# A hybrid encoder step on one core: operand splits later behind their loads, late norms in place, and a final norm by segments

## The chip, the cores and the metric

The kernel runs as one program on one core of one Trainium2 chip. The metric is the device time of one execution in microseconds (us): the median over the runs shown, smaller is better. The engines are TensorE (PE in the profile, with its weight loads as PEld), VectorE (DVE), ScalarE (ACT), GpSimd (POOL) and SyncE (SP), which issues most DMAs.

## The reference

One layer over 2,048 prompt rows and 32 sample rows (T = 2,080 rows in all), float32, d_model 1,024, d_ff 2,816. A mixing part (band attention and gated linear attention on one input projection) is followed by a gated MLP with a causal convolution. Cut to its core:

```
z = (rmsnorm(x) * (1 + scale_m) + shift_m) @ w_in
ya = band_attention(q, k, v, rel_bias)                  # own chunk of 64 rows and 8 before
yb = rmsnorm(gla(q, k, v, log_a)) * silu(gb)            # linear attention, per-token state
merged = sigmoid(gate_a) * (ya @ w_br_a) + sigmoid(gate_b) * (yb @ w_br_b)
x = x + gate_m * rmsnorm(merged @ w_out, g_post_mix)
h = rmsnorm(x, g_pre_ffn) * (1 + scale_f) + shift_f
u = h @ w_up
y = b_dw + sum_j w_dw[j] * shifted(u, j)                # three taps over rows
a, g = split(y, 2)
x = x + gate_f * rmsnorm((gelu(a) * g) @ w_down, g_post_ffn)
```

The outputs are the rows x, the last keys and values, the linear attention's final states and the last rows of u.

## The kernel before

All activations are held transposed, with channels on the 128 partitions and rows along the free axis. Every float32 operand of a matmul is used as two parts: `split` has ACT copy it into a rounded high part, and DVE subtracts that to get the low part (`hi`, `lo`); `mm3` makes three matmuls of each product: hi·hi, hi·lo, lo·hi. So each operand costs a DMA load into a raw tile, an ACT copy and a DVE subtraction before PE can use it.

The stages by time in the profile:

- 0 to about 240 us: modulation vectors and the first norms; to about 1,350: the input projection, linear attention and attention. PE's gaps there are filled by a generator `fill()`: first the gate projections (`dense`, which calls `ahead(i)` as it goes), then `branch_b()`, the merge product yb @ w_br_b in five column blocks of eight m-steps. `branch_b` also loads the next weights: `load_wb(q)` for w_br_b, `load_half` for w_br_a and w_out; each issues its DMA and calls `split` at once.
- about 1,500 to 1,810: eight blocks of 260 rows (`NBLK`, `ND`): `merge` adds both branches, `project` multiplies by w_out. `project` copies each of eight results out of PSUM on ACT (line 1258), squares it (1260 for the first, 1263 after), and calls `step()` between products. `norms`, a generator in `queue`, then makes the residual and the next norm's modulated rows, h, eight channel tiles each, and stores both to DRAM (`x1T`, `h2T`). The last blocks' norms run late, within the feed-forward: `rstd_late` waits for a place among the feed-forward's matmuls, and `hold[0]` keeps it back to a chosen block.
- from 1,810: the feed-forward as Strassen-Winograd products. Rows form three parts p of two segments of 348 to 350 columns. There are twelve units: three for the up-projection (one a part, 22 blocks each), then nine for the down-projection (three parts by three groups of channels, four blocks each). One block (`block(u, m, ...)`) is seven products `prod` of twelve matmuls each (nine where a group has three channel tiles), into two PSUM tiles `ad` and `g`, with ACT copies between (lines 1814 `g`, 1824 `U2`, 1827 `P5`) since a product accumulates onto a copy of another. A block's last two products (`rest_ad`, `rest_g`) run in the next block.
- from 3,206: the final norm of the last part, and the stores.

In the feed-forward all five engines follow the order in which the code is written (`in_order[0]`); before it PE is ordered by hand and a scheduler orders the others, save instructions pinned by `keep_in_program_order`. What decides the written order is `side()`, called between products. It advances `at_step`, runs `run_due()` (work put off by `soon(n, f)`, n steps later), one `step()` of norms, one `hstep()` and up to two `next(wq)`, and last `pend()`, one step of a `post(p)`.

- `hstep()` advances `load_ops`: it loads a unit's fourteen half operands from h, or later from the activations, up to three ahead (two while a `post` is pending), and splits each: lines 1569 (ACT) and 1570 (DVE, a step later).
- `wq` is `weights()`: it loads columns of weights into eight raw buffers, makes their Winograd sums, and splits each: lines 1645 (ACT) and 1650 (DVE, a step later). An engine that comes to a split whose load has not landed waits, with all that is queued behind it.
- `prod` itself calls `next(wq)` or `hstep()` with `run_due()` until both of its operands exist in the written order.
- `post(p)` is the final norm of part p: statistics on PE, then for each of eight channel tiles a multiply (line 1944, DVE), a residual add (1948: POOL for parts 0 and 1), a load of the next residual rows x1, and a store (1871, SP) two steps later. `post(0)` and `post(1)` run inside units 6 and 9; `post(2)` is the end of the program.
- the feed-forward's first weights are split early: `first()`, the `step` of the last `project`, calls `next(wq)`.

The late modulation in `norms` multiplies into a tile of two buffers, whose reuse waits for the store:

```
h2 = d3.tile([128, ND], F32, name="h2", tag="h2", bufs=2)
mul.tensor_mul(h2, o[:, m], r)
```

Of the kernel before, what the change touches and what calls it, by code (L numbers as in the profile page):

```python
# [58 lines left out]
def encoder_step(ctx: ExitStack, tc: tile.TileContext, I, O):  # L59
# [791 lines left out]
    with ExitStack() as st:  # L851
# [219 lines left out]

        def load_half(w, src, k, half):
# [4 lines left out]
            split(w[0][k][:, cs], w[1][k][:, cs], raw)  # L1077

        def load_wb(q):

            for k in (0, 2):
                raw = wt.tile([128, 2, 256], F32, name="wbr", tag="wr")
                nc.sync.dma_start(raw, dap(I["w_br_b"], k * 128 * D + 256 * q, [[D, 128], [128 * D, 2], [1, 256]]))
                split(wb_[q][0][:, k:k + 2], wb_[q][1][:, k:k + 2], raw)
# [10 lines left out]
        def split_y(y, raws):  # L1095
            for k, raw in zip((0, 2), raws):
                split(y[0][:, k:k + 2], y[1][:, k:k + 2], raw)

        def ahead(i):

            if i == 1:
                yb0.append(raw_y(ybT, NB, 0))
            elif i == 2:
                split_y(yb_[0], yb0.pop())
            elif i == 3:
                load_wb(0)

        def branch_b():

            was = iter([(k, half) for half in range(2) for k in range(4)])  # L1110
            for b in range(5):
                cols = slice(NB * b, NB * b + NB)
                for m in range(KD):
                    ms = slice(128 * m, 128 * m + 128)
                    if b == 0 and m in (0, 2, 4):
# [15 lines left out]
                    for k in range(4):  # L1131
# [6 lines left out]
                        if b == 4 and k == 3:  # L1138
                            load_half(wo_, I["w_out"], m // 2, m % 2)

# [93 lines left out]

    def project(b, step):
# [15 lines left out]
        for m in range(KD):  # L1251
# [6 lines left out]
            nc.scalar.copy(o[:, m], p[:, :ND])  # L1258
# [59 lines left out]

    def run_due():
        for f in due.pop(0) if due else ():  # L1320
            f()
# [9 lines left out]
    def norms(b, t0, o, first):  # L1331
# [26 lines left out]
        def modulate(m):  # L1358
            h2 = d3.tile([128, ND], F32, name="h2", tag="h2", bufs=2)
# [27 lines left out]
        for m in range(KD):  # L1387
# [3 lines left out]
            if m < KD - 1:  # L1391
                yield
        if b < NBLK - 2:
# [48 lines left out]

    def sums(p):

        w = WP[p]
        for j in range(4):
# [11 lines left out]
            for i, v in ((0, x), (2, y)):  # L1458
                nc.sync.dma_start(dap(hT, ((4 * p + i) * 512 + 128 * j) * W, [[W, 128], [512 * W, 2], [1, w]]), v[:, :, :w])
            yield  # L1460
# [59 lines left out]
    def load_ops(todo):  # L1520
# [23 lines left out]
        ahead = [0]  # L1544

        def more():
# [63 lines left out]
    def weights():  # L1610
# [5 lines left out]
        at = {}  # L1616
        cur = -1

        def fetch():
            while todo and free and todo[0][0] <= cur + 1:  # L1620
                c, x = todo.pop(0)
                at[c, x] = i = free.pop(0)
                nc.sync.dma_start(raw(i, NK[cols[c][0]]), w_rows(*cols[c], x))
# [5 lines left out]
        def total3(c):  # L1629
            at[c, "S1"], at[c, "S2"] = s1, s2 = free.pop(0), free.pop(0)  # L1630
            at[c, "S3"] = a21 = at.pop((c, "A21"))
            total(c, nc.gpsimd, "tensor_add", s1, a21, at[c, "A22"])
# [37 lines left out]
        for cur in range(len(cols)):  # L1670
            for x in SPLITS if fresh[cur] else WOPS:
# [126 lines left out]
    def block(u, m, prev, side):  # L1798
# [23 lines left out]
        side()  # L1822
        prod(g[:, 0], u, m, "S2", "T2", False)
# [301 lines left out]
```

## Time and profile before

| | us |
|---|---|
| median of three runs | 3239.17 |
| the runs | 3239.17, 3380.43, 3229.4 |
| profiled execution | 3235.16 |
| its span | 3233.5 |
| mean granted TensorE clock in it | 0.986 |

The profile page gives one execution. A row of a group reads: line, engine, operation, output<-input with tile shapes, count, then busy time in us, mean ns of one, and the idle time of the engine before it with what ended most of it. A timeline row gives start and duration in us, and in brackets the idle time before it and its releaser. A row by window gives the stretch, its width, each engine's busy time with its number of instructions, the granted TensorE clock (1.00 is full), the share of the DMA engines' time, and GB/s. A row of waits reads: engine, output and line, what it waited for, then total us, times, and the longest.

### The profile page before, as it was taken

The numbers are of one execution on the slowest core, as the hardware profiler recorded it, in microseconds if no ns is written. First come the engines' busy times: TensorE is split into PE (matmuls) and PEld (weight loads), VectorE is DVE, ScalarE is ACT, GpSimd is POOL, SyncE is SP. The second block draws the span as 40 slices with busy tenths as digits, with TensorE's granted clock in tenths as the row PEclk, the third lists the DMA queues.
The fourth block names the chain that finished last, engine by engine and source line by source line (L and its number), as shares of the span: only waits on it lengthen the run. The fifth ranks groups of instructions, "written<-read, shape, count | busy, mean of one in ns | idle before, by whom it ended". The sixth has DMA issues, their size and how long they took to land. (4 is left out here: it accounts for less than half of the span.)

```text
span 3233.5 us, 57333 instructions
## 1 busy us (share of the span) xinstructions
PE 3081.9 (95%) x19748; PEld 2967.7 (92%) x19748; DVE 2243.7 (69%) x4883; ACT 1655.1 (51%) x3851; POOL 570.2 (18%) x671
## 2 busy tenths in 40 slices
PE   6999999999999999999999899999999999999996
PEld 4899999998999999889999899999999999999986
DVE  6735527774555555665677899888888779887866
ACT  4412224443545555543445555566666556575855
POOL 3102201111111111111444423400000001311011
PEclk8999999999999999999999999999999999999998
DMA  7344434555333333665475676777987667788784
GB/s 222 102 138 129 138 113 128 136 135 137 109 109 107 109 109 105 192 207 159 138 211 177 212 243 209 240 226 209 260 249 209 189 189 237 239 259 264 233 259 142
DMA packets 601365, 580.19 MB, mean 179 GB/s; under 512 B 55761, under 2 KB 529570, under 8 KB 601074
## 3 DMA queue, kind: packets, MB, share of 16 engines
q1 hardware_dynamic: 556386, 528.93, 55.7%
q10 hardware_dynamic: 44432, 47.34, 4.6%
q8 instruction: 155, 2.54, 0.3%
q14 instruction: 136, 1.11, 0.1%
q0 software_dynamic: 256, 0.26, 0.0%
HBM read 388.71 MB, written 187.65 MB: 178 GB/s over the span
## 5 line engine op out<-in xcount | busy, mean ns | idle before, releaser
L78 PE MATMUL pm<-hA,wh 128*128 128x416 f32 x768 | 290.3, 378 | 0.0
L1705 PE MATMUL ad<-hA,hB 128*128 128x350 f32 (+2 forms) x1665 | 288.1, 324 | 1.2 <-ACT work L1827 1.2
L1650 DVE TENSOR_TENSOR hA<-raws,hA 128x512 fp32r<-128x512 f32 (+1 forms) x366 | 259.4, 719 | 21.7 <-ACT hA L1645 21.5
L1705 PEld LDWEIGHTS ad<-hA,hB 128*128 128x128 f32 x1665 | 271.0, 189 | 1.9 <-ACT work L1827 1.8
L79 PE MATMUL pm<-hA,wh 128*128 128x416 f32 x768 | 270.1, 352 | 0.0
L80 PE MATMUL pm<-hA,wl 128*128 128x416 f32 x768 | 269.9, 351 | 0.0
L1705 PE MATMUL ad<-hA,hA 128*128 128x348 f32 (+2 forms) x1410 | 243.8, 325 | 6.0 <-ACT work L1827 5.2
L1627 POOL TENSOR_TENSOR raws<-raws 128x512 f32<-128x512 f32 (+1 forms) x91 | 145.6, 1612 | 542.4 <-DMA raws<-in_w_down_dram 333.5
L1645 ACT ACTIVATE hA<-raws 128x512 fp32r<-128x512 f32 (+1 forms) x366 | 221.4, 617 | 33.5 <-DMA raws<-in_w_up_dram 14.2
L1705 PEld LDWEIGHTS ad<-hA,hA 128*128 128x128 f32 x1410 | 230.0, 190 | 8.0 <-ACT work L1827 6.3
L1705 PE MATMUL g<-hA,hB 128*128 128x350 f32 (+2 forms) x1305 | 228.0, 324 | 3.5 <-DVE hA L1570 2.6
L1705 PEld LDWEIGHTS g<-hA,hB 128*128 128x128 f32 x1305 | 212.6, 189 | 5.9 <-DVE hA L1570 4.2
L1650 DVE TENSOR_TENSOR hB<-raws,hB 128x512 fp32r<-128x512 f32 (+1 forms) x289 | 203.4, 711 | 6.3 <-ACT hB L1645 6.1
L952 POOL TENSOR_SCALAR P<-P,mx 128x640 f32<-128x640 f32 (+5 forms) x136 | 101.3, 745 | 543.1 <-DVE mx L951 282.9
L1705 PE MATMUL ad<-hA 128*128 128x350 f32 (+2 forms) x1116 | 193.6, 323 | 3.4 <-ACT work L1827 3.3
L1645 ACT ACTIVATE hB<-raws 128x512 fp32r<-128x512 f32 (+1 forms) x289 | 174.3, 617 | 36.3 <-DMA raws<-in_w_up_dram 17.3
L1705 PEld LDWEIGHTS ad<-hA 128*128 128x128 f32 x1116 | 180.8, 189 | 4.6 <-ACT work L1827 3.9
L78 PE MATMUL pn<-wh,hA 128*128 128x256 f32 (+1 forms) x624 | 178.0, 285 | 0.0
L79 PE MATMUL pn<-wl,hA 128*128 128x256 f32 (+1 forms) x624 | 177.1, 284 | 0.0
L80 PE MATMUL pn<-wh,hA 128*128 128x256 f32 (+1 forms) x624 | 176.9, 283 | 0.0
L69 ACT ACTIVATE pth<-pp 128x256 fp32r<-128x256 f32 (+1 forms) x288 | 106.0, 373 | 124.4 <-PE pp L1019 114.3
L1814 ACT COPY g<-ad 128x348 f32<-128x348 f32 (+2 forms) x102 | 44.3, 434 | 241.8 <-PE ad L1705 166.1
(461 smaller groups left out, 8815.9 us busy)
## 6 DMA issues: line engine op xcount, KB each, us to landing
raws<-in_w_up_dram SPq DMA_DIRECT2D x220, 256.0 KB, 3.8
raws<-sW SPq DMA_DIRECT2D x176, 256.0 KB, 3.7
sW<-raws SPq DMA_DIRECT2D x88, 256.0 KB, 4.8
raws<-in_w_down_dram SPq DMA_DIRECT2D x80, 256.0 KB, 5.3
wr<-in_w_in_dram SPq DMA_DIRECT2D x76, 256.0 KB, 3.2
sgT<-tx ACTq DMA_DIRECT2D x80, 208.0 KB, 2.7
wa<-in_w_ada_dram SPq DMA_DIRECT2D x64, 256.0 KB, 3.0
keys<-ks SPq DMA_DIRECT2D x128, 128.0 KB, 3.0
```

The lines of the kernel that those rows point to most:

```text
L69: i = nc.scalar.activation(hi, src, AF.Copy)
L78: nc.tensor.matmul(out, ah, bh, start=first and i == 0, stop=False)
L79: nc.tensor.matmul(out, ah, bl, start=False, stop=False)
L80: nc.tensor.matmul(out, al, bh, start=False, stop=last and i == n - 1)
L952: nc.gpsimd.tensor_scalar(P[:m, :tot], P[:m, :tot], mx[:m, 6:7], 1.0, op0=OP.mult, op1=OP.mult)
L1627: getattr(eng, op)(raw(out, n), raw(a, n), raw(b, n))
L1645: act = nc.scalar.activation(hi[:, :n], raw(i, n), AF.Copy)
L1650: nc.vector.tensor_sub(lo[:, :n], raw(i, n), f32(hi[:, :n]))
L1705: nc.tensor.matmul(out[:, :w], l_[:, k], r_[:, k, :w], start=first and k == 0 and i == 0, stop=k == n - 1 and i == 2, skip_group_check=True)
L1814: nc.scalar.copy(g[:, 0, :w], ad[:, 0, :w])
```

## The change

1. `load_half` and `load_wb` put their raw tile in a list; `split_arrived()` splits it at the next m-step of `branch_b`, pinned in program order; `ahead` loads w_br_b at its second call and splits at its third.
2. In the last `project` the first weights' splits are issued after the latest PSUM copy (`issue_after`).
3. In the feed-forward's very first block, product S1×T1 comes before S2×T2.
4. `weights` keeps the first five columns' splits until two steps after their load. `load_ops` keeps each split until three steps after its load, yields less in between, and loads a sum only when it has been stored.
5. The late modulation writes onto its input; late residuals take two steps each; the late norms of the block before last start one block earlier.
6. In `post(0)` and `post(1)` the residual add is on DVE.
7. The end is a new function `finish(2)`: per segment (the second first) statistics, gates, multiplies, adds (two of eight on DVE, six on POOL) and stores; all eight residual tiles are loaded ahead, and the last block's sums are taken by segment.

```diff
         def load_half(w, src, k, half):
...
-            split(w[0][k][:, cs], w[1][k][:, cs], raw)
+            arrived.append((w[0][k][:, cs], w[1][k][:, cs], raw))
...
+        def split_arrived():
+            while arrived:
+                split(*arrived.pop(0), keep=True)
...
         def ahead(i):
...
             elif i == 2:
+                load_wb(0)
+            elif i == 3:
                 split_y(yb_[0], yb0.pop())
-            elif i == 3:
-                load_wb(0)
+                split_arrived()
...
                 for m in range(KD):
                     ms = slice(128 * m, 128 * m + 128)
+                    split_arrived()
...
-            nc.scalar.copy(o[:, m], p[:, :ND])
+            copied[0] = nc.scalar.copy(o[:, m], p[:, :ND]).ins
...
     def run_due():
+        tick[0] += 1
...
-            h2 = d3.tile([128, ND], F32, name="h2", tag="h2", bufs=2)
+            h2 = o[:, m] if in_order[0] else d3.tile([128, ND], F32, name="h2", tag="h2", bufs=2)
...
             if m < KD - 1:
                 yield
+                if in_order[0] and not hold[0]:
+                    yield
...
         def more():
             while ahead[0] < len(todo) and len(raws) < (2 if pending else 3):
+                u, x, j, n = todo[ahead[0]]
+                if UNITS[u][1] is None and x in HT and summed.get(UNITS[u][0], -1) < j + 1:
+                    break
                 load(ahead[0])
+                when[ahead[0]] = tick[0]
                 ahead[0] += 1
...
-            if in_order[0] and i % 2 == 0:
+            if in_order[0] and i % 2 == 0 and i < 4:
                 yield
+            while i not in when or in_order[0] and tick[0] < when[i] + 3:
+
+                yield
+                more()
...
+                while in_order[0] and cur < 5 and tick[0] < born.get((cur, x), -9) + 2:
+
+                    yield
...
+        if not prev:
+
+            prod(ad[:, 1], u, m, "S1", "T1", True)
         prod(g[:, 0], u, m, "S2", "T2", False)
         nc.scalar.copy(U2[:, :w], g[:, 0, :w])
         side()
-        prod(ad[:, 1], u, m, "S1", "T1", True)
+        if prev:
+            prod(ad[:, 1], u, m, "S1", "T1", True)
...
-            add = nc.vector if final and i % 2 else nc.gpsimd
+            add = nc.vector
...
+    def finish(p):
...
+        for s, ps, tag in ((1, psA, "ad"), (0, psG, "g")):
+            split(sh[:, s], sl[:, s], sa[:, s, :o])
+            rs[s] = q = ps.tile([128, 2, 512], F32, name=tag, tag=tag)[:, s, :o]
+            nc.tensor.matmul(q, ones, sh[:, s], start=True, stop=False)
+            nc.tensor.matmul(q, ones, sl[:, s], start=False, stop=True)
+        for s in (1, 0):
+            q = rs[s]
...
+            for i, m in enumerate(ORDER):
+                acc = ACC[p, m]
+                a = acc[:, s, :o]
+                nc.vector.tensor_mul(a, a, q)
+                add = nc.vector if i % 3 == 2 else nc.gpsimd
+                add.tensor_add(a, a, xs[m][:, s, :o])
+                move(p, acc, O["yT"], m, False, s)
...
         if 0 < early[0] < 6:
-            next(wq)
+            with tc.issue_after(copied[0]):
+                next(wq)
...
-            if u == 1 and m == 2:
+            if u == 1 and m == 1:
                 hold[0] = False
...
-    pending.append(post(2))
-    while pending:
-        pend()
+    finish(2)
```

New line numbers of what moved little: 1258 is 1269 in the changed kernel, 1569 is 1598, 1570 is 1599, 1645 is 1677, 1650 is 1682, 1814 is 1849, 1944 is 1988, 1948 is 1992.

Three places show how instructions move. The first is ACT where `branch_b` begins, near 1,330 us: `wbr` is a raw tile of w_br_b, `ybr` one of yb, `pth<-pp` an attention probability tile. Before:

```order
L69 ACTIVATE hB_677<-wbr 128x512 x2
L69 ACTIVATE pth<-pp 128x256
L69 ACTIVATE hB_676<-ybr 128x832 x2
L222 ACTIVATE tx<-pm 128x416
L945 ACTIVATE P,mx<-P,mx 128x256
L948 ACTIVATE P,mx<-F,mx 128x128
```

And now:

```order
L948 ACTIVATE P,mx<-F,mx 128x384
L222 ACTIVATE tx<-pm 128x416
L69 ACTIVATE pth<-pp 128x128
L230 DMA sgT<-tx 128x416
L69 ACTIVATE hB_676<-ybr 128x832 x2
L69 ACTIVATE hB_677<-wbr 128x512 x2
```

Both splits stand some twenty instructions later, behind attention work, and yb's ahead of the weights'.

The second is ACT in the last `project`, near 1,790 us: `oD<-po` is the copy out of PSUM, `hA<-raws` the split of a first feed-forward weight, `hA<-ht` that of rows. Before:

```order
L1569 ACTIVATE hA_105<-ht 128x700
L1645 ACTIVATE hA_104<-raws 128x512
L1258 COPY oD<-po 128x260
L1260 ACTIVATE sa<-po 128x260
L1258 COPY oD<-po 128x260
L1263 ACTIVATE sqD<-po 128x260
```

And now:

```order
L1269 COPY oD<-po 128x260
L1271 ACTIVATE sa<-po 128x260
L1269 COPY oD<-po 128x260
L1274 ACTIVATE sqD<-po 128x260
L1362 ACTIVATE sqD<-oD 128x260
L1269 COPY oD<-po 128x260
L1274 ACTIVATE sqD<-po 128x260
L1362 ACTIVATE sqD<-oD 128x260 x2
L1269 COPY oD<-po 128x260
L1274 ACTIVATE sqD<-po 128x260
L1362 ACTIVATE sqD<-oD 128x260
L1598 ACTIVATE hA_105<-ht 128x700
```

The first split of a weight, ahead of all copies before, now comes behind four of the eight, two rows below this piece.

The third is DVE in the stretch of `post(1)`, near 3,070 us: `work<-work,saF` is the final norm's multiply, `work<-work,ht` the residual add, `hA<-ht` and `hA<-raws` the low parts of rows and weights. Before:

```order
L1650 TENSOR_TENSOR hB_677<-raws,hB_677 128x512
L1944 TENSOR_TENSOR work<-work,saF 128x2x346
L1650 TENSOR_TENSOR ring<-raws,ring 128x512
L1830 TENSOR_TENSOR g<-g,work 128x348
L1650 TENSOR_TENSOR hA_105<-raws_26855,hA_105 128x512
L1944 TENSOR_TENSOR work<-work,saF 128x2x346
L1570 TENSOR_TENSOR hA_104<-ht,hA_104 128x2x348
L1838 TENSOR_TENSOR ad<-ad,work 128x348
```

And now:

```order
L1682 TENSOR_TENSOR hA_105<-raws,hA_105 128x512
L1988 TENSOR_TENSOR work<-work,saF 128x2x346
L1682 TENSOR_TENSOR ring<-raws,ring 128x512
L1992 TENSOR_TENSOR work<-work,ht 128x2x346
L1869 TENSOR_TENSOR g<-g,work 128x348
L1682 TENSOR_TENSOR hA_105<-raws_26839,hA_105 128x512
L1988 TENSOR_TENSOR work<-work,saF 128x2x346
L1599 TENSOR_TENSOR hA_104<-ht,hA_104 128x2x348
L1992 TENSOR_TENSOR work<-work,ht 128x2x346
L1877 TENSOR_TENSOR ad<-ad,work 128x348
```

Each multiply is followed within one or two instructions by its residual add, which stood on POOL before.

More of the change, by code (lines that the diff above doesn't have):

```diff
@@ L1631, in total3 @@
             at[c, "S3"] = a21 = at.pop((c, "A21"))
+            born.update({(c, x): tick[0] + 1 for x in ("S1", "S2", "S3")})
             total(c, nc.gpsimd, "tensor_add", s1, a21, at[c, "A22"])
@@ L1846, in rest_ad @@
                 up_ad(p, m, ad, ya)
+            elif last:
+                for seg in (1, 0):
+                    down_sum(p, grp, m, ad, False, seg)
             else:
```

32 lines of the change are left out of this document (27 added, 5 removed).

## Prediction

> **What bounds the kernel now.** I read the page's head first, then a table of busy time by stage, then PE's timeline at every gap over 1 us, and last what the engines ahead of PE waited for. The first lines show each engine's share and the group of one of ACT's copies out of PSUM.
>
> ```profile
> span 3233.5 us, 57333 instructions
> ...
> PE 3081.9 (95%) x19748; PEld 2967.7 (92%) x19748; DVE 2243.7 (69%) x4883; ACT 1655.1 (51%) x3851; POOL 570.2 (18%) x671
> ...
> L1814 ACT COPY g<-ad 128x348 f32<-128x348 f32 (+2 forms) x102 | 44.3, 434 | 241.8 <-PE ad L1705 166.1
> ```
>
> PE is busy 3081.9 of 3233.5 us. The change keeps every matmul, so only PE's 151.6 idle microseconds and its matmuls at a lowered clock can go, and a gain has to be found in stages where PE waits. The table by stage has window, width, busy time of PE, weight load, DVE, ACT and POOL, then granted clock, DMA share and rate.
>
> ```profile
> core 0: us, PE busy (x) PEld busy (x) DVE busy (x) ACT busy (x) POOL busy (x), PEclk, DMA share, GB/s
> 960.00:1280.00 320.00, 316.88 (x1964) 297.39 (x1964) 162.06 (x619) 161.50 (x485) 56.99 (x77) 1.00 0.36 103
> 1320.00:1500.00 180.00, 166.69 (x1010) 151.39 (x1010) 118.24 (x371) 87.51 (x246) 28.25 (x38) 1.00 0.60 183
> 1785.00:1815.00 30.00, 21.35 (x149) 20.58 (x148) 23.51 (x34) 15.05 (x36) 14.21 (x17) 0.88 0.79 244
> 1855.00:1930.00 75.00, 69.27 (x424) 67.82 (x423) 71.78 (x98) 37.76 (x66) 22.07 (x15) 1.00 0.81 250
> 2118.00:2148.00 30.00, 28.32 (x176) 27.74 (x175) 27.64 (x43) 19.14 (x33) 0.40 (x4) 1.00 0.76 229
> 2174.00:2296.00 122.00, 113.82 (x693) 111.78 (x692) 104.68 (x192) 83.73 (x153) 0.00 (x0) 0.99 0.75 213
> 2360.00:2660.00 300.00, 298.34 (x1857) 297.77 (x1856) 243.85 (x401) 177.52 (x364) 0.26 (x4) 1.00 0.71 206
> 2728.00:2766.00 38.00, 32.35 (x185) 30.62 (x184) 33.51 (x47) 21.46 (x41) 13.63 (x8) 0.96 0.84 260
> 2904.00:2965.00 61.00, 55.31 (x336) 54.49 (x335) 46.98 (x61) 36.82 (x67) 13.71 (x8) 0.97 0.90 291
> 3073.00:3126.00 53.00, 45.06 (x262) 44.24 (x260) 37.18 (x49) 27.79 (x50) 10.54 (x7) 0.94 0.96 291
> 3206.00:3233.00 27.00, 1.67 (x4) 0.98 (x4) 15.98 (x20) 5.22 (x8) 7.89 (x6) 0.58 0.38 118
> ```
>
> The rows 960 and 2360 are calm stretches: PE idles 3.12 of 320 us (1.0%) in the attention and 1.66 of 300 (0.55%) in the feed-forward. Below, idle means what a window has beyond these rates. The change has nothing for calm stretches. PE's own rows at the gaps (start, length, then the idle time before and what ended it):
>
> ```profile
> 1793.28 0.59 PE L78 MATMUL po<-mhl,hA 128*128 128x260 f32 x1 [5.79 <-ACT sa L1260]
> 1894.12 2.20 PE L1705 MATMUL ad<-hA 128*128 128x350 f32 x12 [2.90 <-ACT work L1827]
> 2185.44 7.56 PE L1705 MATMUL ad<-hA,hA 128*128 128x348 f32 x36 [2.45 <-ACT work L1827]
> 2747.83 1.23 PE L1705 MATMUL g<-hA,hA 128*128 128x348 f32 x6 [2.78 <-DVE hA L1570]
> 2926.66 3.49 PE L1705 MATMUL g<-hA 128*128 128x346 f32 x12 [4.38 <-ACT work L1824]
> 3083.31 3.23 PE L1705 MATMUL g<-hA,hA 128*128 128x348 f32 x12 [4.34 <-ACT work L1824]
> 3106.05 2.08 PE L1705 MATMUL g<-hA,hB 128*128 128x348 f32 x12
> 3111.73 3.57 PE L1705 MATMUL g<-hB,hA 128*128 128x348 f32 x12 [3.60 <-ACT g L1814]
> ```
>
> The releaser is nearly always an ACT copy out of PSUM that takes 0.43 us by its group. It is late because ACT, which works in program order, stood at a split whose load had not landed:
>
> ```profile
> 1792.04 0.63 ACT L1645 ACTIVATE hA<-raws 128x512 fp32r<-128x512 f32 x1 [5.88 <-DMA raws<-in_w_up_dram]
> ...
> 3081.62 0.78 ACT L1569 ACTIVATE hB<-ht 128x696 fp32r<-128x696 f32 x1 [5.08 <-DMA ht<-aT]
> ```
> ```profile
> ACT hA L69 <- DMA wr<-in_w_out_dram: 9.7, 4, 4.7
> ```
> ```profile
> DVE h L1361 <- DMA h2T<-h: 8.8, 4, 3.6
> ```
>
> So PE waits for ACT, and ACT for a transfer. The last row is DVE's: the late modulation waits four times, 8.8 us in all, for the store that frees its two-buffer tile.
>
> **The change part by part.** The sum stands against the profiled execution, 3235.16 us, of which 3233.5 is the span. The median of the runs shown is 3239.17, 0.1% above.
>
> 1. Merge weights later (1320 to 1500). The splits of `load_half` and `load_wb` move one m-step, four `mm3` groups, behind their loads; no instruction is added, and SP's loads stand where they did. Idle is 13.31 − 1.76 = 11.6 us. ACT's four waits above for these weights are 9.7 us, but other waits in this stage (the softmax chain's) stay, so the ends are 0 and 11.6; I take half, 5.8. The step's matmuls hide the delay. Without that cover a weight would be late for its matmul, by no more than the 4.7 us of the longest wait.
>
> 2. First weights behind the projection's copies, and block 0's first two products swapped (1785 to 1815). Before, a weight split that waits 5.88 us stands ahead of the PSUM copies L1258 and L1260, and PE idles 5.79. After, copies stand ahead of it. The load is issued as before, and the split waits only for its own data. The swap puts product S1×T1 where PE waited for L1814. Idle is 8.65 − 0.17 = 8.5; the clock costs at most 0.12 × 30 = 3.6. Ends 0 and 12.1. I take 7: the 5.79 less 0.8 for two copies, and 2 for the swap and the clock.
>
> 3. Row splits three steps behind loads, and the first five columns' weights two steps behind. A step is a product of twelve matmuls, 12 × 300 / 1857 = 1.94 us in the calm stretch. Where ACT stood up to 5 us at a load, it now does the copies queued behind it first. This covers 1855 to 1930 (75 − 69.27 − 0.41 = 5.3 idle; I take 3, the 2.90 gap), the first block of the second unit, 2118 to 2148 (1.5; half, 0.8), and the unit boundary 2728 to 2766 (5.65 − 0.21 = 5.4, with the clock at most 6.9; I take 4, the 2.78 gap and 1.2 of the rest, since some waits there end on DVE and not on ACT). If the cover fails, a product demands its operand first, and the wait turns up as PE waiting for L1570 or L1650.
>
> 4. Late modulation in place, residuals over two blocks, norms one block earlier (2174 to 2296). The 8.8 us of waits for a store go, because the tile now written is the one read; only the store of the residual, at least eight steps old, must be done. Idle 8.18 − 0.67 = 7.5, clock at most 1.2, ends 0 and 8.7. I take 6.5: the pieces are the same in number, and DVE at 104.68 of 122 us is close enough to full that one late copy may stay.
>
> 5. Residual add on DVE, and row splits three steps behind (2904 to 2965, 3073 to 3126). The rows are the present DVE multiply and POOL add, and the waits of SP's store:
>
> ```profile
> 3070.82 0.87 DVE L1944 TENSOR_TENSOR work<-work,saF 128x692 f32<-128x692 f32 x1
> ```
> ```profile
> 3100.03 1.55 POOL L1948 TENSOR_TENSOR acc<-acc,ht 128x692 f32<-128x692 f32 x1 [4.57 <-DMA ht<-x1T]
> ```
> ```profile
> SPq L1871 <- POOL acc L1948: 7.2, 4, 2.4
> ```
>
> Sixteen adds at 0.87 put 13.9 us on DVE, which idles 14.0 and 15.8 us in the two windows. That is hidden as long as the x1T load is there; if not, everything DVE does for the next products stands behind the add. In return SP's stores, which held later loads for 7.2 us, come 0.7 us sooner each (1.55 against 0.87). The gaps go by the row splits: idle 5.69 − 0.34 = 5.35 with at most 1.8 of clock, and 7.94 − 0.29 = 7.65 with at most 3.2. Twelve matmuls take 2.08 us, but 3.49, 3.23 and 3.57 behind the three gaps above 3.5 us, so these three cost 4.05 us more than their idle time. I take 5 of 7.15 and 7.5 of 10.85.
>
> Shorter gaps differ: behind 2.90 us twelve matmuls took 2.20, hardly more, but behind 2.45 us thirty-six took 7.56, 1.7 over three products of 1.94. So a gap only shortened may still cost clock, and I return that term in proportion. [...]
>
> 6. The end by segments.
>
> ```profile
> 3204.57 0.53 DVE L1838 TENSOR_TENSOR ad<-ad,work 128x348 f32<-128x348 f32 x1 [0.94 <-PE ad L1705]
> ...
> 3217.84 1.54 POOL L1948 TENSOR_TENSOR acc<-acc,ht 128x696 f32<-128x696 f32 x1 [40.84 <-DVE acc L1944]
> ...
> 3224.20 2.17 POOL L1948 TENSOR_TENSOR acc<-acc 128x696 f32<-128x696 f32 x1 [0.19 <-DVE acc L1944]
> 3225.74 1.37 DVE L1948 TENSOR_TENSOR acc<-acc,ht 128x696 f32<-128x696 f32 x1
> ```
>
> Before, four of eight adds were on DVE and the last compute ends at 3227.1. After, DVE has six gate steps, sixteen multiplies and four adds of half width, 26 × 0.53 = 13.8 us, and POOL twelve half adds, between 12 × 0.77 = 9.2 and 12 × 1.09 = 13.0 us (half of 1.54, half of 2.17). POOL's first add started at 3217.84; about eight steps of the chain ahead of it lie on half the width, 0.53 against 0.87, which is 2.7 us, of which I count 2, so POOL starts at 3215.8 and ends between 3225.0 and 3228.8: 2.1 us better to 1.7 worse. I take 1, DVE being done sooner.
>
> Sum: 5.8 + 7 + 3 + 0.8 + 4 + 6.5 + 5 + 7.5 + 1 = 40.6, and 3235.16 − 40.6 = 3194.6: I forecast **3194 us**, 1.4% under the median. All the upper ends together are 11.6 + 12.1 + 5.3 + 1.5 + 6.9 + 8.7 + 7.15 + 10.85 + 2.1 = 66.2, or 3169.0.
>
> **The rivals.** *A. Transfers are the bound and waits only move.* For it: 3073 to 3126 has a DMA share of 0.96 at 291 GB/s, the highest rate of the table, so 15.4 MB in that window need at least 51 us, and the term of 7.5 shrinks to 2. If half of the terms in parts 1 and 3 (13.6) also return as products that wait for L1570 and L1650, 6.8 more are lost: 3194.6 + 5.5 + 6.8 = 3207, and with part 5's other window halved, 3209. Against it: the other windows stand at 0.60 to 0.90. [...]
>
> *B. DVE stands at the residual's load (slower than before).* In place of POOL, DVE waits w for x1T at each of the 16 adds. Its work and waits, 13.9 + 16w, beyond its 29.8 us of idle time fall on PE, and part 5's 12.5 are lost: 3194.6 + 12.5 + 13.9 − 29.8 + 16w = 3191.2 + 16w. At the 4.57 us of the row above it is 3264; it decides from w = 3.0, where it passes 3239.17, and is 2% slower from w = 7.1. Against it: the row is the longest of POOL's, whose other adds mostly waited for the multiply.
>
> *C. Everything named goes.* The upper ends give 3169.0; a little less for A's lower bound in the last window still ends under 3174.4, the line of 2%.
>
> **How the numbers follow.** The forecast case (3180 to 3203) has 0.55, A 0.25 at 3209, C 0.15 at 3169, B 0.05 at 3264. The range runs from C's end with 4 us for stores at the end, 3165, to A with its terms all lost in parts 1 and 3 (3209 + 6.8 = 3216) and 6 us for a new wait, 3222; it leaves out B and the edges, under 2 in 10. A measurement of this kernel tells about 2% from no change. Faster by over 2% is C and a fringe of the forecast, 0.17; slower by over 2% is B beyond w = 7.1, and unknown mishaps, 0.04; within 2% the rest, 0.79.
>
> **What would show it.** Right: at the end of the last projection PE waits under 1.5 us; ACT's waits for raws and ht in 1855 to 1930 and in the first blocks of units fall to a third; DVE has no wait for h2T; the two windows of the final norm idle under 4 us together beyond the calm rate and their clock is 1.00. Wrong: PE waits for L1599 or L1682 (the splits' new lines) in place of ACT copies, a DVE wait for x1T, POOL as the last engine at the end, or calm stretches that idle more than 1.0 and 0.55%.

## The result

| | us |
|---|---|
| changed kernel, median of 4 runs | 3205.95 (3200.21 to 3210.27) |
| kernel before, median of 4 runs | 3235.91 |
| ratio, with its 95% interval | 0.9912 (0.9898 to 0.9926) |
| profiled execution of the changed kernel | 3200.21, span 3198.5 |

One run of the kernel before took 3380.43 us, 4.7% more than its fastest, and the ratio leaves it out. The kernel is 0.9% faster, some 28.5 us (0.0088 × 3235.91), where 1.4% and 40.6 us were forecast. The profiled execution of the changed kernel is the fastest of its four: its span is 35.0 us below that of before, of which about 6 are the run's luck. Its head and its table by stage, the same places as before (window, width, busy time of PE, weight load, DVE, ACT, POOL, clock, DMA share and rate):

```profile
span 3198.5 us, 57346 instructions
...
PE 3075.2 (96%) x19748; PEld 2963.9 (93%) x19748; DVE 2248.1 (70%) x4913; ACT 1654.4 (52%) x3856; POOL 550.0 (17%) x663
```
```profile
1320.00:1493.00 173.00, 166.63 (x1019) 152.81 (x1018) 122.15 (x375) 89.85 (x249) 30.26 (x38) 1.00 0.66 199
1773.00:1806.00 33.00, 23.86 (x186) 22.62 (x184) 28.29 (x42) 17.82 (x43) 17.27 (x20) 0.94 0.76 233
1848.00:1923.00 75.00, 70.42 (x423) 69.26 (x422) 70.01 (x100) 38.41 (x67) 25.32 (x16) 0.98 0.79 254
...
2168.00:2279.00 111.00, 110.17 (x687) 109.30 (x686) 100.21 (x181) 77.75 (x145) 0.00 (x0) 1.00 0.78 226
...
2887.00:2940.00 53.00, 49.10 (x308) 48.52 (x307) 44.62 (x65) 31.97 (x57) 0.00 (x0) 1.00 0.94 311
3048.00:3095.00 47.00, 43.76 (x262) 42.96 (x260) 37.53 (x56) 27.26 (x49) 0.00 (x0) 0.96 1.05 328
3172.00:3198.00 26.00, 4.70 (x21) 3.29 (x19) 18.10 (x37) 6.98 (x16) 11.28 (x12) 0.61 0.33 110
```

Three places idle less, as meant: PE idles 6.4 us in place of 13.3 around the merge, 0.8 in place of 8.2 in the late norms, and 3.9 and 3.2 in place of 5.7 and 7.9 in the final norm's stretches. Two did not: PE idles 9.1 us at the last projection and 4.6 in blocks 3 to 7 (8.7 and 5.7 before, with the clock of the latter now at 0.98). PE's rows at these two places, and ACT's ahead of them:

```profile
1800.55 0.50 PE L1847 MATMUL g<-hA 128*128 128x512 f32 x1 [2.62 <-ACT sqD L1274]
1805.87 3.56 PE L1740 MATMUL ad<-hA,hA 128*128 128x350 f32 x12 [4.82 <-ACT g L1849]
...
1879.57 3.06 PE L1740 MATMUL g<-hA,hA 128*128 128x350 f32 x12 [2.53 <-ACT g L1849]
```
```profile
1804.68 0.79 ACT L1598 ACTIVATE hA<-ht 128x700 fp32r<-128x700 f32 x1 [4.18 <-DMA ht<-h2T]
...
1874.37 1.15 ACT L1677 ACTIVATE hA<-raws 128x512 fp32r<-128x512 f32 x2 [5.13 <-DMA raws<-in_w_up_dram]
```

The gap of 5.79 us ahead of the projection's copies is gone, and one of 4.82 stands at block 0: ACT waits for rows there, where it waited for a weight. In blocks 3 to 7 it waits for a weight as before.

The program is fixed, so the same instruction can be timed in every kernel. The next table is worked out from the starts of ACT's copies in the timelines: `yh<-py` in the attention, `oD<-po` in the projections, and a block's first copy `g<-ad` in the feed-forward (line 1814 before, 1849 after). "Others" are the experiments below in which the place stands as in the changed kernel, and give the spread between runs. "The whole merge stage" runs from the 41st of the 64 attention copies to the first projection copy, and holds the two rows above it.

| stretch | before | changed | others | forecast gain |
|---|---|---|---|---|
| five attention units at the merge weights | 54.59 | 46.35 | 46.37 to 46.40 | 5.8 with the next row |
| the unit behind, a sample's cached keys | 9.11 | 10.82 | 11.21 to 16.31 | |
| the whole merge stage | 286.63 | 281.09 | 280.59 to 287.48 | |
| last project's start in block 6 to block 1 (merge included) | 77.30 | 77.32 | 77.14 to 79.74 | 7 |
| blocks 1 to 4 | 42.11 | 40.61 | 40.61 | 0 |
| blocks 4 to 8 | 59.63 | 61.22 | 61.16 to 62.75 | 3 |
| blocks 22 to 24 | 29.13 | 29.40 | 28.77 to 30.30 | 0.8 |
| blocks 24 to 33, late norms | 134.35 | 124.11 | 124.11 to 124.16 | 6.5 |
| blocks 66 to 68, unit boundary | 35.65 | 33.63 | 32.94 to 33.98 | 4 |
| blocks 68 to 80 | 152.84 | 150.60 | 150.37 to 150.75 | 0 |
| blocks 80 to 83, first part's norm | 47.94 | 44.38 | 43.43 to 45.72 | 5 |
| blocks 92 to 95, second part's norm | 51.69 | 45.59 | 46.19 to 48.29 | 7.5 |
| block 101 to the end | 37.5 | 33.9 | 33.6 to 35.0 | 1 |

One experiment (u_steps) took 36.53 in blocks 66 to 68, with nothing edited there; its granted clock was 0.86 in that stretch, against 0.95 in the changed kernel. It is left out of that row.

Starts counted from the beginning of the program vary far more than these stretches. Block 0's first copy starts at 1805.38 us in the changed kernel, and at 1810.3 to 1817.5 in the six experiments whose edits act only behind it (u_inplace, u_steps, u_rows, u_post, w_all, w_8). So where an expectation below names such a start, it is judged by stretches.

### The profile page after: what moved, and what is told of

Read it like the earlier page. It is cut to its first block, busy times and chain, and to the rows that moved or that the text cites. A ratio compares the mean times of both kernels' runs of the same rounds, so it can differ in the third digit from the quotient of the medians.

```text
span 3198.5 us, 57346 instructions
## 1 busy us (share of the span) xinstructions
PE 3075.2 (96%) x19748; PEld 2963.9 (93%) x19748; DVE 2248.1 (70%) x4913; ACT 1654.4 (52%) x3856; POOL 550.0 (17%) x663
## 5 line engine op out<-in xcount | busy, mean ns | idle before, releaser
L1740 PE MATMUL ad<-hA,hB 128*128 128x350 f32 (+2 forms) x1566 | 271.3, 324 | 6.7 <-ACT work L1866 3.4
L1682 DVE TENSOR_TENSOR hA<-raws,hA 128x512 fp32r<-128x512 f32 (+1 forms) x368 | 257.5, 708 | 16.5 <-ACT hA L1677 15.9
L1740 PEld LDWEIGHTS ad<-hA,hB 128*128 128x128 f32 x1566 | 255.2, 190 | 7.8 <-ACT work L1866 4.3
L1740 PE MATMUL ad<-hA,hA 128*128 128x348 f32 (+2 forms) x1362 | 235.0, 325 | 5.5 <-ACT g L1849 4.8
L1740 PEld LDWEIGHTS ad<-hA,hA 128*128 128x128 f32 x1362 | 222.3, 190 | 7.0 <-ACT g L1849 5.1
L1740 PE MATMUL ad<-hA 128*128 128x350 f32 (+2 forms) x1263 | 218.3, 323 | 4.4 <-ACT work L1866 4.3
L1740 PEld LDWEIGHTS ad<-hA 128*128 128x128 f32 x1263 | 204.5, 188 | 6.2 <-ACT work L1866 6.1
L1682 DVE TENSOR_TENSOR hB<-raws,hB 128x512 fp32r<-128x512 f32 (+1 forms) x287 | 203.5, 716 | 4.0 <-ACT hB L1677 3.9
```

What stands on the lines that cost most here:

```text
L1682: nc.vector.tensor_sub(lo[:, :n], raw(i, n), f32(hi[:, :n]))
L1740: nc.tensor.matmul(out[:, :w], l_[:, k], r_[:, k, :w], start=first and k == 0 and i == 0, stop=k == n - 1 and i == 2, skip_group_check=True)
```

## The experiments

Each is the changed kernel with one edit. Times are ratios to the kernel before.

**u_merge: part 1 undone.**

```diff
-            arrived.append((w[0][k][:, cs], w[1][k][:, cs], raw))
+            split(w[0][k][:, cs], w[1][k][:, cs], raw)
...
```

The splits of `load_wb` and the order in `ahead` are also those of before.

> The changed kernel with part 1 undone: the merge weights are split at once behind their loads. Theory L (each part's gain is made at its place and stays): the first copy of the first project block, at 1515.9 us now and 1522.0 before, returns to about 1522, block 0's first copy moves from 1805.4 to about 1811, and the time rises by about 6 us (ratio to the kernel before about 0.993). Theory G (what is gained here is taken back at the last project, where block 0 waits for row loads that have their own chain): block 0's first copy moves by 2 us or less and the time by 2 or less.

0.9925 (0.9905 to 0.9945), an interval that overlaps the changed kernel's, so the stretches decide. The five attention units take 59.06 us, 12.7 more than with part 1 and 4.5 more than before, so the run is not quite the old state. The gap of before is back there. PE's row of before, then of this run:

```profile
1365.66 0.33 PE L1019 MATMUL pp<-ident,P 128*128 128x128 f32 x1 [2.95 <-POOL P L952]
```
```profile
1367.83 0.47 PE L1019 MATMUL pp<-ident,P 128*128 128x128 f32 x1 [4.06 <-POOL P L952]
```

The whole merge stage takes 290.63 us, 7.0 more than the mean of the kernels with part 1 (283.6). From block 6 to block 1 it takes 77.14, 0.2 to 2.6 us less than the kernels with part 1 unchanged there, so little of that is taken back at block 0: theory L holds for these stretches. Block 0's first copy, at 1813.19, says nothing, since kernels with part 1 have it there too. But the unit behind takes 9.24 us, as before, where every kernel with part 1 takes 10.8 to 16.3. So part 1 also made a new wait, which the next experiment looked at.

**x_ck4: yb's last loads behind the cached keys' load.**

```diff
+                with tc.issue_after(lastck[0]) if n == NB and b == 4 else ExitStack():
                     nc.sync.dma_start(raw, dap(src, k * 128 * T + n * b, [[T, 128], [128 * T, 2], [1, n]]))
```

> The changed kernel with one pair of yb's loads (its last column block) put behind the load of a cached key tile on SP, which they stand ahead of since the merge weights come later. Theory K (the pair slows that tile's transfer, and PE's wait for its split, 0.7 us in one run and up to 4.0 with the clock lost behind it in others, is what the later weights give back): PE's wait for the cached keys near 1,380 us is under 0.3 us, and the stretch between the attention copies on both sides of it (1377.0 to 1387.8 now, 10.8; 11.3 to 16.3 in other runs of the same code) takes 9 to 10. Rival: the tile is late for another reason and the stretch stays at 10.8 or more.

0.9908 (0.9889 to 0.9926); the unit takes 11.94 us, within what the others take, and PE still waits 1.78 us for the keys. ACT's split of the tile, and SP's issue of its load, first in the changed kernel, then here:

```profile
1379.94 0.63 ACT L69 ACTIVATE keys<-ck 128x512 fp32r<-128x512 f32 x1 [2.59 <-DMA ck<-in_cache_kT_dram]
```
```profile
1374.41 1.16 SPq L882 DMA_DIRECT2D ck<-in_cache_kT_dram  x2
```
```profile
1384.11 0.63 ACT L69 ACTIVATE keys<-ck 128x512 fp32r<-128x512 f32 x1 [3.68 <-DMA ck<-in_cache_kT_dram]
```
```profile
1379.93 1.23 SPq L884 DMA_DIRECT2D ck<-in_cache_kT_dram  x2
```

By the marks set beforehand (under 0.3 us for the wait, 9 to 10 for the unit) the rival holds, and not theory K. From issue to split the tile takes 4.2 us in place of 5.5, as theory K has it. But the edit also moved the load itself: its issue stands 0.1 us ahead of the attention copy that begins the unit (1380.06), where it was 2.6 us ahead (1376.98). So the run doesn't settle whether the pair of loads is the cause.

**u_first: the order of the first weight splits undone; u_swap: block 0's products in the old order.**

```diff
-            with tc.issue_after(copied[0]):
-                next(wq)
+            next(wq)
```
```diff
-        if not prev:
-
-            prod(ad[:, 1], u, m, "S1", "T1", True)
```

> The changed kernel with part 2's order undone: the first weight split may again stand ahead of the last project's PSUM copies. Theory L (the copies' order is worth its gap): PE's gap of 5.8 us ahead of the first copy is back and block 0's first copy comes 5 us later or more, at 1810 or later; time up by 5. Theory G (block 0's start is set by the chain from POOL's weight sums over the residual adds and SP's stores to the row loads, and the copies' order only moves the wait): the gap is back, but block 0's first copy comes under 2 us later than 1805.4, and the time changes by less than 2 us.

> The changed kernel with block 0's first two products in the old order (S2xT2 first). Theory L (the swap hides the copy): PE waits for the copy and then once more, block 1's first copy comes 1.5 to 2 us later than 1820.45. Theory G (the wait there is for the row split ahead of the copy, which no order of products behind the copy hides, because both products need that copy or late rows): block 1's first copy within 0.7 us of 1820.45.

u_first: 0.9917 (0.9899 to 0.9935). The projection's first copy comes 6.1 us later against the block before than in the changed kernel, but the stretch to block 1 takes 79.74 us, at the end of the others' range: of the 6.1 us, 0 to 2.6 are left. u_swap: 0.9914 (0.9895 to 0.9932), the stretch 78.18, in the middle of the range. So neither edit is worth what was forecast, as theory G has it. The next two runs tested the cause that it named.

**v_sums: POOL's first weight sums behind the residual adds; v_store: x1's stores issued by ACT.**

```diff
-            with tc.issue_after(copied[0]):
+            with tc.issue_after(copied[0]), tc.issue_after(added[0]):
```
```diff
-                nc.sync.dma_start(x1T[128 * m:128 * m + 128, t0:t0 + ND], o[:, m])
+                (nc.scalar if b == NBLK - 2 and not in_order[0] else nc.sync).dma_start(
+                    x1T[128 * m:128 * m + 128, t0:t0 + ND], o[:, m])
```

> The changed kernel with one thing added: POOL makes the first three weight sums only behind the latest residual add traced by then, so three more residual adds stand ahead of the sums. Theory G (sums hold the adds, the adds hold SP's x1 stores, the stores hold the row loads): the stores that were issued at 1789.0 come at about 1785, the row loads behind them 3 to 4 us earlier, PE's gap at block 0 (4.82 us) falls to 1 to 2, and block 0's first copy comes at 1801 to 1803; time down by 3 to 5 us. Rival (weights bind block 0): the sums end about 3 us later, so the first products wait for weights and block 0's first copy does not come earlier than 1805.

> The changed kernel with the x1 stores of the second to last block's residuals (in the last project) issued by ACT in place of SP, so that SP's row loads no longer stand behind a store that waits for POOL's residual add. Theory G (SP's stores hold the row loads, and these set block 0): the row loads for block 0 come 3 us earlier or more, ACT's wait for h2T of 4.2 us at block 0's first copy falls under 2, and the stretch from the last project's first copy to block 1's first copy, 40.7 us now and 34.9 before, takes 36 to 38. Rival (the chain from weight loads over POOL's sums is as late, as the run with later sums had it): the same stretch within 1 us of 40.7.

v_sums: 0.9925 (0.9901 to 0.9948), the stretch 80.22 us, so theory G's gain of 3 to 5 us did not come. v_store: 0.9907 (0.9887 to 0.9928), 79.37. From the projection's first copy to block 1's, v_store takes 38.2 us (40.7 in the changed kernel; theory G said 36 to 38), but the first copy itself is 4.6 us later. PE's and ACT's rows of v_store:

```profile
1790.96 0.58 PE L78 MATMUL po<-mhl,hA 128*128 128x260 f32 x1 [4.57 <-ACT sa L1271]
...
1813.09 3.87 PE L1741 MATMUL ad<-hA,hA 128*128 128x350 f32 x12 [1.05 <-ACT g L1850]
```
```profile
1790.24 0.38 ACT L1269 COPY oD<-po 128x260 f32<-128x260 f32 x1 [4.14 <-DMA x1T<-oD]
...
1806.51 0.79 ACT L1599 ACTIVATE hA<-ht 128x700 fp32r<-128x700 f32 x1 [1.89 <-DMA ht<-h2T]
```

The wait for rows falls from 4.18 to 1.89 us and PE's gap at block 0 from 4.82 to 1.05, in part only because ACT comes later. Counted from block 6's first copy, though, that split of rows starts 57.5 us in, against 61.6 in the changed kernel, so the stores did hold the row loads. But a later split of rows waits 1.46 us more, and ahead of the projection's copies ACT waits again. In v_sums one of the eight adds still stood behind the sums, and ACT waited 4.85 us for rows. Three edits at three links of this stage, and each time the wait turned up at another link.

What all kernels share is the row split: in all fourteen profiles the last long wait of ACT ahead of block 0's first copy is at one, and that copy starts 62.0 to 64.7 us after block 6's (63.1 before, 62.2 in the changed kernel). What holds the row loads is open. In the changed kernel SP has one more candidate, which no run tested: a weight load between the row loads waits 2.3 us for a weight sum's store.

**u_inplace and u_steps: the two halves of part 4.**

```diff
-            h2 = o[:, m] if in_order[0] else d3.tile([128, ND], F32, name="h2", tag="h2", bufs=2)
+            h2 = d3.tile([128, ND], F32, name="h2", tag="h2", bufs=2)
```
```diff
-                if in_order[0] and not hold[0]:
-                    yield
...
-            if u == 1 and m == 1:
+            if u == 1 and m == 2:
```

> The changed kernel with the late modulation back in its two-buffer tile, the two steps a residual and the earlier norms kept. Theory S (the store's release of the two buffers was the wait): DVE's waits for that store are back, 4 to 9 us, and blocks 26 to 33 take 4 to 7 us longer than now. Rival T (the gain came from spreading the residuals over two steps): under 2 us longer.

> The changed kernel with the late residuals in one step each and the norms of the block before last one block later, as before; the modulation stays in place. Theory S: blocks 26 to 33 take 1 to 3 us longer than now. Rival T: 5 us longer or more.

Single runs, 3213.11 and 3223.22 us, so the stretch decides. Blocks 24 to 33 take 127.62 us with the tile back and 127.26 with the steps back, 3.5 and 3.1 more than 124.11. Together they are 6.6 of the 10.2 us gained; no run undid both, so it is not shown where the rest comes from. In blocks 26 to 33, the stretch named beforehand, they take 1.6 and 3.0 us more (97.24 in the changed kernel): the norms start one block earlier now, and the tile's other 1.9 us come in blocks 24 to 26. DVE's wait for the store is back in u_inplace, half as long as before:

```profile
DVE h L1376 <- DMA h2T<-h: 4.2, 2, 2.7
```

So theory S named a wait that is there, but its 4 to 7 us are missed, and by the stretch as it was named rival T's mark (under 2 us) is met; the steps gave about as much as the tile.

**u_rows: row splits at once; u_post: the residual add on POOL.**

```diff
-            while i not in when or in_order[0] and tick[0] < when[i] + 3:
+            while i not in when:
```
```diff
-            add = nc.vector
+            add = nc.gpsimd
```

> The changed kernel with the row splits no longer kept three steps behind their loads (they yield once per half operand as before). Theory L (the delay is what emptied ACT's waits): the stretches of the final norm lose what they gained: blocks 80 to 83 and 92 to 95 take 3 and 5 us longer than now, and the unit boundaries 66 to 68 about 2 longer; time up by 8 to 10 us. Rival (the residual add on DVE gave that gain, by freeing SP's stores sooner): under 3 us in all three places.

> The changed kernel with the residual adds of parts 0 and 1 back on POOL. Theory L (the add's engine matters little, row splits made the gain): blocks 80 to 83 and 92 to 95 within 2 us of now. Rival: SP's stores wait for POOL again, and those blocks take 4 us longer or more together.

u_rows also yields before every second half operand, as before the change. 0.994 (0.9923 to 0.9957): blocks 66 to 68 take 35.83 us, 68 to 80 152.38, 80 to 83 46.48 and 92 to 95 50.66, which is 2.2, 1.8, 1.6 and 3.4 above the means of the changed kernel and the others (33.6, 150.6, 44.9, 47.3), 9.0 in all. The long waits of before are back; one of them in PE's and ACT's rows of u_rows:

```profile
3070.38 3.68 PE L1740 MATMUL g<-hA,hA 128*128 128x348 f32 x12 [4.17 <-ACT work L1862]
```
```profile
3068.69 0.79 ACT L1598 ACTIVATE hB<-ht 128x696 fp32r<-128x696 f32 x1 [4.99 <-DMA ht<-aT]
```

u_post: 0.9905 (0.9886 to 0.9924), the two stretches at 44.95 and 47.18, on the means. So the delay of row splits (with the yields that go with it) made most of the gain, 5.0 of the 7.4 us by the means in the final norm's two stretches, and the engine of the residual add makes no difference that shows.

**w_all and w_8: the weights' delay for more columns.**

```diff
-                while in_order[0] and cur < 5 and tick[0] < born.get((cur, x), -9) + 2:
+                while in_order[0] and cur < 66 and tick[0] < born.get((cur, x), -9) + 2:
```

> The changed kernel with the two steps between a weight's load and its split kept for all up-projection columns, not the first five alone. Theory M (blocks 3 to 7 gained nothing because the weights' splits there are past the rule's end): ACT's 5.1 us wait for raws near 1874 falls under 2, and blocks 4 to 8 (61.2 us now) take 58 to 59.5. Rival (the transfers are late there, at a DMA share of 0.79, whatever ACT does): PE waits for the weights themselves and blocks 4 to 8 take 60.5 to 63.

> The changed kernel with the two steps between a weight's load and its split kept for the first eight columns, not five. Theory M2 (the delay pays where ACT stands at a load that has not landed, and costs where weights are made just in time, as it did from block 8 on with all columns): the gap of 2.5 us ahead of block 5's second product is gone, blocks 4 to 8 take 59 to 60 us (61.2 now), blocks 9 to 22 stay at 13.5 to 13.7 each, and the time falls by about 2 us, to a ratio of 0.990 to 0.992 to the kernel before. Rival (the eighth column already binds a product): one of blocks 7 to 9 takes over 15.5 us and nothing is gained.

w_all: 0.9995 (0.9984 to 1.0005), the whole gain lost. Blocks 4 to 8 take 59.4 us, as theory M had it, but from block 8 to block 22 it takes 222.57, 32.5 more than the changed kernel's 190.07. The window behind block 8 in the changed kernel and in w_all, and one of w_all's PE rows:

```profile
1923.00:2043.00 120.00, 119.83 (x743) 119.01 (x742) 111.00 (x152) 66.19 (x115) 44.86 (x26) 1.00 0.66 207
```
```profile
1930.00:2050.00 120.00, 112.60 (x661) 109.54 (x660) 92.45 (x132) 57.84 (x102) 32.54 (x24) 0.96 0.55 183
```
```profile
1972.34 1.88 PE L1740 MATMUL ad<-hA,hB 128*128 128x350 f32 x10 [1.69 <-DVE hB L1682]
```

The clock stands at 0.96 there, PE works 661 matmuls in place of 743, and it waits for DVE's low part of a weight: the product needs its operand before the rule lets it go. w_8 (`cur < 8`) does it for eight columns: blocks 4 to 8 take 59.62 us and blocks 8 to 22 190.74, and the ratio is 0.9912 (0.9896 to 0.9928). The gap of 2.53 us is gone, and blocks 4 to 6 take 4.7 us less than in the changed kernel, but block 7 takes 17.50 in place of 14.38: at its end PE waits 2.12 us for DVE's low part of a weight. That is the mark that was set for the rival, a product that the eighth column already binds. What is gained at the place does not show in the whole, and no kernel here beats the changed one by more than its interval.

## Why the prediction was right in direction and range, and wrong in places

The measured 3205.95 us lies in the range, but 3 us outside the forecast case (3180 to 3203), and nearer to rival A's 3207 and 3209 than to 3194. That the sum held as well as it did is in part luck. By the means of the changed kernel and the others, parts 1, 2, 3 and 5 gave some 24 us less than forecast together, and parts 4 and 6 with two stretches for which nothing was forecast some 10 more.

- Part 1, "I take half, 5.8": the mechanism was right, but the row that priced it was the wrong one, and the size came near by luck. The 9.7 us for `w_out` lie behind the five units, and ACT waits as long for these weights now, only later. What went is its waits for w_br_a (5.1 us), yb (3.0) and w_br_b (1.9), none of which is left. ACT's rows of waits in 1320 to 1500 us, before and now:

```profile
ACT hA L69 <- DMA wr<-in_w_br_a_dram: 5.1, 6, 1.5
```
```profile
ACT hA L69 <- DMA wr<-in_w_out_dram: 10.4, 5, 3.3
```

  The five units gained 8.2 us, in all kernels alike, and the unit behind gave back 1.7 to 7.2. Over the whole merge stage the gain is 5.5 us in the profiled run and 3.0 by the mean, where single runs lie between 6.0 gained and 0.9 lost. The prediction gave the delay's own cost as nothing and priced no load that stands beside the moved ones on SP.
- Part 2, "I take 7: the 5.79 less 0.8 for two copies, and 2 for the swap and the clock": the step that failed. The stretch takes 77.30 before and 77.32 now. "The split waits only for its own data" was true, but the rows were as late as the weights, and the gap of 4.82 us at block 0, with 3.56 us for twelve matmuls behind it, took the place of the first. The row that warned stood in ACT's timeline of before, just ahead of block 0's copy:

```profile
1812.51 0.79 ACT L1569 ACTIVATE hA<-ht 128x700 fp32r<-128x700 f32 x1 [2.07 <-DMA ht<-h2T]
```

- Part 3, blocks 3 to 7, "I take 3, the 2.90 gap": wrong. The late operand there is a weight of a column past the fifth, to which the delay doesn't apply. From block 4 to block 8 PE idles as long as before (4.5 and 4.6 us); the 1.6 us that it became longer are PE's busy time, 56.6 in place of 55.1 us for the same 338 matmuls, with one stretch of 3.41 us at half clock, of which the last section tells. w_8, which applies the delay to three more columns, gains 4.7 us in blocks 4 to 6 and loses 3.1 in block 7. The unit boundary gave 2.0 of 4: the 2.78 gap is gone, but PE now waits there for L1682, the sign that was set for being wrong, and for longer. Undoing the row delay (u_rows) brings back a gap of 2.79 in place of this one:

```profile
2718.85 2.13 PE L1740 MATMUL ad<-hA,hB 128*128 128x348 f32 x10 [3.25 <-DVE hB L1682]
```

  Blocks 22 to 24 gave nothing of 0.8. Two stretches for which nothing was forecast gained: blocks 68 to 80 gave 2.2, and u_rows shows that it is the same delay; blocks 1 to 4 gave 1.5, in every kernel alike, where PE has no gap left. The last fits the weights' delay, which was not undone by itself.
- Part 4, "I take 6.5": 10.2, mis-sized, and 1.5 more than the window's idle time and clock together (8.7). Over blocks 24 to 33 PE's idle time fell by 7.1 us (7.69 to 0.62) and its busy time by 3.2 (126.66 to 123.49). Of the latter the slow matmuls behind the gap of 2.45 us were 1.7 (7.56 against 5.8); where the other 1.4 went no row shows.
- Part 5, "I take 5 of 7.15 and 7.5 of 10.85": 3.0 and 4.4 by the means (3.6 and 6.1 in the profiled run). The row splits made most of it, as argued, and the residual add on DVE was free, as argued. Rival B's wait, in DVE's table of waits over both stretches, is one of 0.2 us:

```profile
DVE work L1992 <- DMA ht<-x1T: 0.2, 1, 0.2
```

- Part 6, "I take 1": 3.6 in the profiled run, 2.5 to 3.9 over all. The computing gave what was counted: from the last product's end to the end of the last add it takes 20.0 us in place of 21.2. The other 2.5 came behind the last add, where nothing was counted and only stores are left: from there to the end of the span it takes 3.9 us in place of 6.4. Ahead of it, POOL's first add starts 8.2 us after the last product in place of 11.9, where 2 of these 3.7 were counted.

```profile
3173.04 1.59 PE L1740 MATMUL g<-hA,hB 128*128 128x348 f32 x9
...
3182.81 0.80 POOL L2026 TENSOR_TENSOR acc<-acc,ht 128x348 f32<-128x348 f32 x1 [38.31 <-DVE acc L2024]
...
3193.69 0.92 POOL L2026 TENSOR_TENSOR acc<-acc,hA 128x348 f32<-128x348 f32 x1
```

POOL is the last engine, which was set as a sign of being wrong, and its 11.28 us of adds lie between the two ends given, 9.2 and 13.0. The end by segments was not undone by itself.

Of the signs of being right, only one came out whole: DVE has no wait for h2T in the late norms. At the last projection PE waits 4.82 us and not under 1.5, ACT's waits for weights in blocks 3 to 7 fell from 14.7 to 12.1 us and not to a third, and the final norm's windows idle 6.6 us beyond the calm rate and not under 4, with clocks of 1.00 and 0.96.

Rival A, that waits only move, was right about parts of two of the six parts (the second, and blocks 3 to 7 of the third) and about what stands behind part 1. Its reason, that transfers are the bound, is not shown, and its floor did not hold: the 15.4 MB that it gave at least 51 us now move in 47, at 328 GB/s.

## What to carry to other kernels

When an in-order engine waits for a load, put the work that others wait for ahead of it; how far behind its load the split may stand is bounded by the product that needs it, and the same kind of delay that gave 9.0 us on rows cost 32.5 where weights came just in time. Before counting a gap as gained, list every wait in the stage that ends within a few us of it: at the last projection each edit brought up another wait, and none moved the end. Time the same instruction in several kernels, and first see how far a stretch varies between runs of the same code: where it agrees to 0.05 us, as in blocks 24 to 33, it settles what a ratio with an interval of 0.3% can't, but starts from the beginning of the program varied by 12 us.

## What was not expected of the hardware

A short gap's price in clock did not go by its length here. Behind gaps of 2.90 and (in the changed kernel) 2.60 us twelve matmuls took 2.20 and 2.17 us, but behind 2.24 us thirty-six took 7.49, where three products of 1.94 are 5.8:

```profile
2905.83 2.17 PE L1740 MATMUL ad<-hA 128*128 128x346 f32 x12 [2.60 <-ACT work L1866]
...
3058.29 7.49 PE L1740 MATMUL ad<-hA,hB 128*128 128x348 f32 x36 [2.24 <-ACT work L1866]
```

The records of the granted clock show where it was paid. In the feed-forward of these profiles the clock is 1.00 or 0.50, each stretch at 0.50 is 3.41 us long or twice that, and all changes of a profile stand on one grid of 3.41 us. Here the changed kernel is cut by its grid, two windows around each of the gaps above:

```profile
2901.18:2904.59 3.41, 2.05 (x13) 1.76 (x12) 2.10 (x3) 1.19 (x2) 0.00 (x0) 1.00 1.08 376
2904.59:2908.01 3.42, 2.18 (x14) 2.18 (x15) 3.06 (x5) 3.41 (x8) 0.00 (x0) 1.00 1.02 367
...
3054.77:3058.18 3.41, 1.28 (x8) 1.00 (x7) 1.86 (x3) 2.22 (x5) 0.00 (x0) 1.00 1.09 347
3058.18:3061.60 3.42, 3.31 (x11) 3.31 (x12) 3.42 (x7) 2.14 (x5) 0.00 (x0) 0.50 1.07 354
```

The gap of 2.60 us is cut in two, PE idles 1.36 and 1.24 us in its windows, and the clock stays at 1.00. The gap of 2.24 lies nearly whole in one window, PE idles 2.13 us in it, and the next window is at 0.50. Before, the gap of 2.45 lay whole in one window and cost clock, and that of 2.90 was cut into 1.61 and 1.29 and cost none. Over the feed-forward of all fourteen profiles (1,820 to 3,170 us), a window at full clock with 1.9 us of idle time or more was followed by one at 0.50 in 54 of 54 cases, and one with less in 3 of 5,412 (after 1.58, 1.82 and 1.86 us of idle time). So in these traces the window ahead of half clock need not be idle throughout: PE idled 2.13 of its 3.41 us here. The price came by the window, some 1.7 us by the rows of 7.49 and 7.56, and not in proportion to the gap: in part 5's two windows there were three such stretches before and one in the changed kernel.

An elementwise operation on DVE took over three times as long beside one on POOL: the same add of 128x260 took 1.51 us while POOL made the weight sums, and 0.42 us after, in the changed kernel's last projection.

```profile
1785.36 1.51 DVE L1363 TENSOR_TENSOR sa<-sa,sqD 128x260 f32<-128x260 f32 x1
...
1790.92 0.42 DVE L1363 TENSOR_TENSOR sa<-sa,sqD 128x260 f32<-128x260 f32 x1
```
```profile
1785.13 2.90 POOL L1658 TENSOR_TENSOR raws<-raws 128x512 f32<-128x512 f32 x2 [0.31 <-DMA raws<-in_w_up_dram]
```

The rows show that the two ran at the same time; why the add took longer, no run here shows.
